# An attention kernel with bias: the first pair's bias chunk loaded last and added after the scores, and the second pair's first head copied straight from PSUM

## The chip, the cores and the metric

The kernel runs on one core of a Trainium2 chip. The metric is the device time of one execution in microseconds (us). A core has a matrix engine (PE, with its weight loads shown apart as PEld), VectorE (DVE), ScalarE (ACT), GpSimd (POOL) and SyncE (SP), each with its own instruction stream in a fixed order, and 16 DMA engines that serve the queues of all of them. Matmul results go to PSUM; everything else lies in SBUF.

## The reference

```python
batch, n_heads, seq_len, head_dim = 4, 8, 1024, 64
scores = (1 / sqrt(head_dim)) * q @ k.T + bias      # bias: [1, 1, 1024, 1024]
attn = exp(scores - max) / (sum(exp(scores - max)) + 1e-8)
out = attn @ v
```

All tensors are float32. There are 32 heads; one bias matrix serves all of them.

## The kernel before

**Tiling.** Heads are worked in 16 pairs. A *slot* is one query chunk c (128 queries) of one head h: a 128x1024 block of scores in one of three PSUM places (`pl`, two banks each). There are 256 slots. For 237 of them ACT takes the exponential of the whole block into a bf16 tile `E` (line 258); for 19, listed in `PLAN`, DVE works it out in six steps (lines 263 to 298). PE then multiplies it with V (`av`, line 312) into a PSUM bank `po` that collects up to 7 results, with V's 65th column of ones giving the sums, and DVE divides and stores (`evac`, lines 315 to 333).

**Scores that stay in PSUM.** A place keeps its sum from slot to slot. The first slot in a place (`start`) adds the bias to the score; each next slot of the same chunk adds its own head's score and takes away the one before. For that, an even head's operands `ke` and `qe` hold the head's own 64 rows and, in the other 64, those of the head before, negated in q; odd heads use `ko` and `qo` of the whole pair. `fill_half` (line 233) writes one bank: four matmuls of bias ("b", the bias chunk against 8 times the identity) or of scores ("s"). `fill` (line 246) writes both banks. Slots 0, 1 and 2 are the first head's chunks 0 to 2 in places 0 to 2.

**From memory to operands.** For each pair, K, Q and V are loaded by GpSimd's DMAs, which cast to bf16 (`load_k`, `load_q`, `load_v`, lines 141 to 167). PE transposes K and Q into a PSUM tile `px` under one of two tags, `xa` and `xb` (`transposes`, line 182), shared with the `po` banks. DVE copies `px` into `ko` or `qo` (`copy_out`, line 195), and from these the 64-row halves are copied into `ke` and `qe` (`double`, line 203; by DVE, GpSimd or, in later pairs, by DMA). V is copied into `vall` (line 493).

**The start** (lines 335 to 392) is written out by hand. Pair 0's q (three chunks), K (two halves) and bias chunk 0 come as float32 through SP's and ACT's queues: q and K's halves on SP, the bias on ACT. GpSimd clears `qz[0]` and `qs` (lines 350, 351; 64x1024 each) and then issues bias chunks 1 and 2, K and Q of pairs 1 and 2, and V of pair 0. DVE casts q and K's first half, ACT casts the bias and K's second half. PE transposes, DVE copies `qz` and `ko`. The bias matmuls of slot 0 go ahead of its scores, and its exponential runs as two halves; the bias matmuls of slot 1 stand between the two score halves of slot 0.

**The rest** is ordered by a planner in the kernel's own Python (lines 394 to 814). It keeps a clock for each engine (`t_pe`, `t_act`, `t_dve`, `t_pool`, in its own nanoseconds, from 9300, 9900, 9600 and 9000), estimates of each step's cost and of each load's landing (`raw_at`, `vland_at`, `t_dma`), and takes at each step what can begin first; work waiting for DVE lies in `dve_q` as (time ready, priority, cost, action), and a smaller priority goes first. What it writes out is a fixed order for each engine: on the chip an instruction waits for its data, and everything behind it on that engine waits too. GpSimd's loads after the start wait until the load five places earlier has landed (`issue`, line 463; the `tick` copies at line 468).

Transposes of a pair's piece are a candidate for PE (lines 646 to 675); behind them `run` (line 665) queues `copy_out` and then `doubles` (line 511), and frees the tag when the whole copy is done. Pair 1's first pieces are K (all 8 chunks) and Q (3 chunks); its even head is head 2, whose slots are 6, 7 and 8.

Of the kernel before, what the change touches and what calls it, by code (L numbers as in the profile page):

```python
# [11 lines left out]
ALU = mybir.AluOpType  # L12
# [4 lines left out]
def kernel(  # L17
# [13 lines left out]
    nc = tc.nc  # L31
    B, H, S, D = q.shape
# [6 lines left out]
    qf = q.rearrange("b (g t) (p c) d -> (b g) p t (c d)", t=2, p=P)  # L39
# [13 lines left out]
    C0 = 3  # L53
# [36 lines left out]
    slots = []  # L90
# [72 lines left out]
    def load_v(pr):  # L163
        lands[pr, "v"] = vland.tile([P, 2, NCH, D], BF, name="v16")
        nc.gpsimd.dma_start(out=lands[pr, "v"].rearrange("p t c d -> p t (c d)"),  # L165
                            in_=vf[pr].rearrange("p t c d -> p t (c d)"))
        return lands[pr, "v"][:1, 1, NCH - 1, D - 1:]
# [14 lines left out]
    def transposes(pr, which, c0, n, tag, px=None):  # L182
        if px is None:
            px = ps_x.tile([P, n, P], BF, tag=tag, name="px")
        for c in range(n):
            if (pr, which, c0) in raws:
                nc.tensor.transpose(px[:, c, :], raws[pr, which, c0][:, c].rearrange("p t d -> p (t d)"), ident[:])  # L187
                continue

            for t in range(2):  # L190
                nc.tensor.transpose(px[t * D:(t + 1) * D, c, :], lands[pr, which, c0][:, t, c, :], ident[:],  # L191
                                    tile_position=(0, t * D))
        return px
# [9 lines left out]
    def double(pr, which, c0, n, part, w):  # L203
# [7 lines left out]
        else:  # L211
            w.tensor_scalar(to[("qe", "qe", "qs", "qz")[part]][rows, cs, :], t["qo"][rows, cs, :], -1.0, 1.0,
                            op0=ALU.mult, op1=ALU.mult)

    def negate(pr):

        t = (raws[pr, 0, 0] if 0 in BESIDE else lands[pr, 0, 0]).rearrange("p t c d -> p (t c d)").rearrange("p (c x) -> p c x", x=P)
        nc.vector.tensor_scalar(t, arrs[pr]["qo"][:], -1.0, 1.0, op0=ALU.mult, op1=ALU.mult)
        return t
# [10 lines left out]
            return t["ko"], t["qz"] if pr in first_pair else t["qs"]  # L230
        return (t["ko"], t["qo"]) if h % 2 else (t["ke"], t["qe"])

    def fill_half(s, b, what):

        x, c, h, start = slots[s]
        kk, qq = operands(s)
        for i in range(4):
            kc = 4 * b + i
            to = places[x][:, b, i * P:(i + 1) * P]
            if what == "b":  # L240
                nc.tensor.matmul(to, braw[:, c, :].rearrange("p (kp kc) -> p kc kp", kc=NCH)[:, kc, :], ident8[:],  # L241
                                 start=i == 0, stop=False, skip_group_check=True)
            else:
                nc.tensor.matmul(to, kk[:, kc, :], qq[:, c, :], start=False, stop=True, skip_group_check=True)  # L244

    def fill(s):
        for what in "bs" if slots[s][3] and s > 1 else "s":
            for b in range(2):
                fill_half(s, b, what)

    etile = {}

# [82 lines left out]
    with tc.manual_schedule():  # L335

        half = NCH // 2
        nc.sync.dma_start(out=q0f[:], in_=qf[0][:, :, :C0 * D].rearrange("p t (c d) -> p t c d", d=D))
        nc.scalar.dma_start(out=b0f[:], in_=bf_[:, 0, :])
        for i in range(2):  # L340
            nc.sync.dma_start(out=k0f[:, :, i * half:(i + 1) * half].rearrange("p t c d -> p t (c d)"),
                              in_=kf[0][:, :, i * half * D:(i + 1) * half * D])
        nc.vector.memset(zeros, 0.0)
        nc.vector.memset(warm[:], 0.0)
        nc.vector.memset(sgn[:D, :], -1.0)
# [2 lines left out]
        make_identity(nc, ident[:])  # L348

        nc.gpsimd.memset(qz[0][D:, :, :], 0.0)  # L350
        nc.gpsimd.memset(qs[D:, :, :], 0.0)
        for c in (1, 2):
            load_b(c)
        load_k(1)
# [1 line left out]
        load_k(2)  # L356
        load_q(2, slice(0, NCH))
        load_v(0)
        for i in range(10):
            nc.tensor.matmul(places[2][:, 0, :], zeros[:, :P], zeros, start=True, stop=True)  # L360

# [7 lines left out]
        nc.vector.tensor_scalar(ident8[:], ident[:], 1.0 / scale, None, op0=ALU.mult)  # L369
        nc.vector.tensor_copy(qr0.rearrange("p c t d -> p t c d"), q0f[:])  # L370
        nc.vector.tensor_copy(kr0[0].rearrange("p c t d -> p t c d"), k0f[:, :, :half])
        nc.scalar.copy(braw[:, 0, :], b0f[:])
        nc.scalar.copy(kr0[1].rearrange("p c t d -> p t c d"), k0f[:, :, half:])

        pq = transposes(0, 0, 0, C0, "xa")
        pk = transposes(0, 1, 0, half, "xb")
        pk2 = places[2].bitcast(BF)[:, 1, :half * P].rearrange("p (c x) -> p c x", x=P)
        nc.vector.tensor_scalar(t0["qz"][:D, :C0, :], pq[:D], 1.0, None, op0=ALU.mult)
        copy_out(0, 1, 0, half, pk)
        for i in range(2):  # L380
            fill_half(0, i, "b")
        transposes(0, 1, half, half, None, px=pk2)
        copy_out(0, 1, half, half, pk2)
        copy_out(0, 0, 0, C0, pq)
        fill_half(0, 0, "s")
        exp(0, 0, 1)
        for i in range(2):
            fill_half(1, i, "b")
        fill_half(0, 1, "s")
        exp(0, 1, 1)  # L390
        double(0, 1, 0, NCH, 1, nc.vector)
        double(0, 0, 0, C0, 1, nc.vector)

# [38 lines left out]
        TR, SWITCH = 56, 190  # L432
        LATE, QCOST = 2, 4400
        flight = []
        LAG, AVG = 7, 247
        E1, E2 = 1400, 1700
        free_lands, loads, loads_v = set(), list(range(EARLY, NP)), []
# [70 lines left out]
            else:  # L508
                bias_at[pr] = issue(0, E2, 5, load_b, pr)

        def doubles(pr, which, c0, n, t2, urgent):
            if not which and pr >= EARLY:
                def run(t3):
                    to = negate(pr)
                    last = parts(pr, 0)[-1]
                    for x in parts(pr, 0):
                        key = (("qe", "qe1", "qs", "qz")[x], pr + (x == 1), 0)
                        sp_q.append((t3 + 430 + L_DVE, lambda t4, x=x, key=key: copy(pr, x, key[0][:2], to, key, t4, x == last)))
                dve_q.append((t2, 0.2 if urgent else 2, 430, run))
                return  # L520
            for x in parts(pr, which):
                key = (("ke", "ke1")[x], pr + (x == 1)) if which else (("qe", "qe1", "qs", "qz")[x], pr + (x == 1), c0)
                if which and (pr >= EARLY or x == 1 and pr >= 2):
                    sp_q.append((t2 + L_DVE, lambda t3, x=x, key=key: copy(pr, x, "ke", arrs[pr]["ko"], key, t3)))
                elif which or urgent:
                    cost = (130 if which else 240) + 38 * n

                    def run(t3, x=x, key=key, cost=cost):
                        double(pr, which, c0, n, x, nc.vector)
                        ready[key] = t3 + cost + L_DVE  # L530
                    dve_q.append((t2, (0.2, 0.4, 0.4, 0.2)[x] if urgent else 2, cost, run))
                else:
                    double(pr, which, c0, n, x, nc.gpsimd)
                    pool(t2)
                    ready[key] = pool(0, 125 * n + 100) + 300
# [40 lines left out]
        def pe_cands():  # L576
# [69 lines left out]
            if pieces:  # L646
                pr, which, c0, n = pieces[0]
                need = need_at[pr, which, c0]
                ring = pr + linked(pr) - RING
                lag = len([s for s in avq[:NE] if s in e_at])  # L650
                if ((pr, which, c0) in raw_at and next_fill >= need - AHEAD and (ring < 0 or last_slot[ring] < next_fill)
                        and (lag < 4 or need - next_fill < 8)):
                    f, tag = min((x_free[y], y) for y in x_free)
                    r = max(f, raw_at[pr, which, c0])
                    cost = n * TR + SWITCH * (pr < EARLY or which not in BESIDE)
                    urgent = need - next_fill < 12
                    if r < 1e11:
                        def do(t, pr=pr, which=which, c0=c0, n=n, tag=tag, cost=cost):
                            x_free[tag] = 1e12
                            pieces.pop(0)  # L660
                            px = transposes(pr, which, c0, n, tag)
                            if pr < EARLY and which == 0 and c0 == 0:
                                freed(pr, t)

                            def run(t2):
                                copy_out(pr, which, c0, n, px)
                                done = t2 + 60 * n + (180 if which else 300)
                                x_free[tag] = done + L_DVE
                                if which:
                                    ready["ko", pr] = done + L_DVE  # L670
                                else:
                                    ready["qo", pr, c0] = done + L_DVE
                                doubles(pr, which, c0, n, done, urgent)
                            dve_q.append((t + cost + L_PE, 0 if urgent else 2, 60 * n + (180 if which else 300), run))
                        out.append((max(t_pe, r), cost, do, 2 if next_fill < need - 12 else 0.5, 0))
            return out

# [167 lines left out]
```

## Time and profile before

| what | value |
|---|---|
| median of 3 runs | 232.69 us (232.66 to 232.89) |
| profiled execution | 232.87 us, span 230.8 us |
| PE / PEld busy | 222.4 us (96%) / 209.8 us (91%) |
| ACT busy | 221.3 us (96%), x242 |
| DVE busy | 197.3 us (85%) |
| POOL busy | 64.5 us (28%) |
| mean granted PE clock | 0.997 |
| DMA | 29.75 MB, mean 129 GB/s |

The span runs from the first to the last instruction of the core. A row of a timeline or of a group gives start and length in us, the engine, the source line, the operation and its tiles (output <- input), the count, and in brackets the idle time ahead of it and what ended it. The chain of waits gives the work that ended last, each piece with its start and length; "issue" is time in which the engine waited for nothing that the profile shows. A DMA row gives the queue: q0 is GpSimd's, q1 is SP's and q10 is ACT's. The busy share of a queue can go over 100%, since packets overlap. PE's busy time is modelled and overlaps, so a busy PE is not PE at its peak.

Where the prediction speaks of single starts, of packets or of landings, they are the trace's records of single instructions, packets and semaphores.

### The profile page before, as it was taken

Reading aid. Unit: us, or ns where it says so; the run is one execution under the profiler, and the core shown is the slowest. Engines: PE = TensorE matmul, PEld = TensorE weight load, DVE = VectorE, ACT = ScalarE, POOL = GpSimd, SP = SyncE. Lnnn points to the kernel's source line nnn. Section 1 sums busy time; section 2 is a strip of 40 time slices with the busy share of each in tenths; the row PEclk is TensorE's granted clock in tenths of the full one; section 3 lists DMA queues with packets and bytes.
Section 4 is the critical chain, followed back from the end, with each engine's and each line's share of the span. In section 5 each row is a group of like instructions: output and inputs, shape, how many; then the busy total and the mean of one; then the engine's idle time right before and its main releaser. Section 6 shows DMA issues by size and latency. Waiting matters only on the chain.

```text
span 230.8 us, 10695 instructions
## 1 busy us (share of the span) xinstructions
PE 222.4 (96%) x4671; PEld 209.8 (91%) x4671; DVE 197.3 (85%) x294; ACT 221.3 (96%) x242; POOL 64.5 (28%) x115
## 2 busy tenths in 40 slices
PE   6999999999999999999999999999999999999993
PEld 2779998999999999998999999999998999999992
DVE  3595678799988997989889789899999899999993
ACT  3799999999999999999999999999999999999994
POOL 8816655167444444313364010000000000000000
PEclk9999999999999999999999999999999999999998
DMA  6999999999999999989899864111111112112212
GB/s 201 212 205 225 216 228 213 195 120 121 161 193 150 146 178 153 176 193 147 140 253 196 186 123 114 38 37 43 43 36 48 45 43 65 53 26 71 65 37 63
DMA packets 55645, 29.75 MB, mean 129 GB/s; under 512 B 31856, under 2 KB 51952, under 8 KB 55600
## 3 DMA queue, kind: packets, MB, share of 16 engines
q0 software_dynamic: 30336, 14.06, 49.0%
q1 hardware_dynamic: 24832, 14.43, 22.6%
q8 instruction: 36, 0.59, 1.0%
q10 hardware_dynamic: 432, 0.59, 0.9%
q14 instruction: 9, 0.07, 0.1%
HBM read 29.36 MB, written 8.39 MB: 164 GB/s over the span
## 4 chain that ended last, share of the span: by engine, by line
PE 36%; ACT 28%; issue 13%; DMA 11%; DVE 7%; POOL 3%; SPq 1%; DVEq 0%; ACTq 0%; POOLq 0%
ACT E L258 28%; PE pl L244 21%; PE po L312 10%; DMA v<-in_v_dram 6%; DMA k<-in_k_dram 4%; PE px L191 2%; PE pl L241 2%; DVE ob L322 2%; DVE dt L290 1%; DVE dy L275 1%; DVE de L295 1%; SPq L694 1%; POOL k L145 1%; POOL q L155 1%; DMA out_dram<-ob 1%
## 5 line engine op out<-in xcount | busy, mean ns | idle before, releaser
L258 ACT ACTIVATE E<-pl 128x1024 bf16<-128x1024 f32 (+1 forms) x238 | 218.1, 1124 | 1.9 <-PE pl L244 1.7
L312 PE MATMUL po<-vall,E 128*128 128x65 bf16 x1896 | 92.0, 194 | 0.7 <-ACT E L258 0.7
L312 PEld LDWEIGHTS <-E 128*128 128x128 bf16 x1896 | 77.5, 98 | 1.8 <-ACT E L258 1.1
L244 PE MATMUL pl<-qo,ko 128*128 128x128 bf16 x1024 | 77.0, 219 | 1.2 <-ACT E L258 0.6
L244 PEld LDWEIGHTS <-ko 128*128 128x128 bf16 x1160 | 69.6, 98 | 4.4 <-issue 1.2
L244 PE MATMUL pl<-qe,ke 128*128 128x128 bf16 x888 | 66.1, 219 | 0.6
L244 PEld LDWEIGHTS <-ke 128*128 128x128 bf16 x888 | 53.4, 98 | 3.4
L275 DVE TENSOR_SCALAR dy<-pl 128x1024 int32<-128x1024 f32 x19 | 23.2, 1222 | 3.4 <-PE pl L244 2.4
L322 DVE TENSOR_TENSOR ob<-po,rs 128x448 f32<-128x448 f32 (+2 forms) x40 | 23.3, 581 | 2.7 <-DMA out_dram<-ob 0.8
L284 DVE SCALAR_TENSOR_TENSOR dt<-df 128x1024 f32<-128x1024 f32 x19 | 23.2, 1220 | 0.3
L295 DVE SCALAR_TENSOR_TENSOR de<-dy,dt 128x1024 uint16<-128x1024 int32 x19 | 23.2, 1219 | 0.1
L287 DVE SCALAR_TENSOR_TENSOR df<-dt,df 128x1024 f32<-128x1024 f32 x19 | 23.1, 1219 | 0.1
L290 DVE SCALAR_TENSOR_TENSOR dt<-df,dt 128x1024 f32<-128x1024 f32 x19 | 23.1, 1219 | 0.1
L138 POOL DMA_DIRECT2D q<-in_q_dram x18 | 16.1, 898 | 5.8 <-PE po L312 4.2
L165 POOL DMA_DIRECT2D v<-in_v_dram x16 | 11.3, 704 | 12.0 <-DVE rs L320 7.5
L199 DVE COPY ko<-px 128x1024 bf16<-128x1024 bf16 (+1 forms) x16 | 10.7, 671 | 4.4 <-PE px L191 4.1
L201 DVE TENSOR_SCALAR qo<-px,sgn 128x1024 bf16<-128x1024 bf16 (+2 forms) x18 | 12.4, 687 | 2.1 <-PE px L187 1.7
L320 DVE RECIPROCAL rs<-po 128x7 f32<-128x7 f32 (+3 forms) x42 | 8.2, 195 | 7.0 <-PE po L312 6.8
L280 DVE TENSOR_SCALAR df<-dy 128x1024 f32<-128x1024 uint16 x19 | 13.0, 687 | 0.1
L241 PE MATMUL pl<-ident,braw 128*128 128x128 bf16 x136 | 11.5, 228 | 0.1
L145 POOL DMA_DIRECT2D k<-in_k_dram x15 | 10.7, 711 | 2.6 <-PE pl L244 1.0
L493 DVE COPY vall<-v 128x1024 bf16<-128x1024 bf16 x16 | 7.0, 438 | 4.3 <-DMA v<-in_v_dram 4.2
(55 smaller groups left out, 124.9 us busy)
## 6 DMA issues: line engine op xcount, KB each, us to landing
v<-in_v_dram POOLq DMA_DIRECT2D x16, 256.0 KB, 6.3
k<-in_k_dram POOLq DMA_DIRECT2D x15, 256.0 KB, 6.1
out_dram<-ob SPq DMA_DIRECT2D x35, 96.0 KB, 3.3
ke<-ko SPq DMA_DIRECT2D x22, 128.0 KB, 4.2
out_dram<-ob SPq DMA_DIRECT2D x40, 64.0 KB, 2.2
q<-in_q_dram POOLq DMA_DIRECT2D x18, 128.0 KB, 4.6
out_dram<-ob SPq DMA_DIRECT2D x68, 32.0 KB, 3.0
qe<-q SPq DMA_DIRECT2D x17, 128.0 KB, 4.1
```

The lines of the kernel that those rows point to most:

```text
L138: nc.gpsimd.dma_start(out=t[:, :, y, :], in_=(qf, kf)[x][pr][:, y].rearrange("p (c d) -> p c d", d=D))
L145: nc.gpsimd.dma_start(out=t.rearrange("p t c d -> p t (c d)"), in_=kf[pr])
L241: nc.tensor.matmul(to, braw[:, c, :].rearrange("p (kp kc) -> p kc kp", kc=NCH)[:, kc, :], ident8[:], start=i == 0, stop=False, skip_group_ ...
L244: nc.tensor.matmul(to, kk[:, kc, :], qq[:, c, :], start=False, stop=True, skip_group_check=True)
L258: nc.scalar.activation(e[:, i:i + n].rearrange("p b x -> p (b x)"), places[slots[s][0]][:, i:i + n].rearrange("p b x -> p (b x)"), ACTF.Ex ...
L275: w.tensor_scalar(t["y"][:], places[slots[s][0]].rearrange("p b x -> p (b x)"), scale * LOG2E * 65536.0, 127.0 * 65536.0, op0=ALU.mult, op ...
L284: w.scalar_tensor_tensor(t["t"][:], t["f"][:], -G, t["f"][:], op0=ALU.add, op1=ALU.mult)
L287: w.scalar_tensor_tensor(t["f"][:], t["t"][:], Q, t["f"][:], op0=ALU.mult, op1=ALU.add)
L290: w.scalar_tensor_tensor(t["t"][:], t["f"][:], V, t["t"][:], op0=ALU.add, op1=ALU.mult)
L295: w.scalar_tensor_tensor(etile[s].bitcast(U16).rearrange("p c q -> p (c q)"), t["y"][:], 1.0 / 512.0, t["t"][:], op0=ALU.mult, op1=ALU.add)
L312: nc.tensor.matmul(po[:, j + i, :], etile[s][:, kc, :], vall[:, slots[s][2] % VR, kc, :], start=j + i + kc == 0, stop=kc == NCH - 1, skip_ ...
L322: nc.vector.tensor_tensor(ob[:, :n, :], po[:, :n, :D], rs[:, :n, :].to_broadcast([P, n, D]), op=ALU.mult)
```

## The change

Loads: K's first half moves to ACT's queue, ahead of everything there; SP's queue takes q, K's second half, and then bias chunk 0 in two halves of 512 columns. The cast of the bias is split in the same way and goes behind that of K's second half on ACT. The clearing of `qs` goes behind the seven loads on GpSimd.

Slots 0 to 2: the score matmuls come first and the bias matmuls second, and slot 0's exponential is one instruction over both banks. Slot 1's bias matmuls leave the hand-written start and stand in its own fill.

Pair 1: its K and first Q piece are copied from PSUM into the 64 rows of `ke` and `qe` directly (`direct`); the whole copies into `ko` and `qo` are queued once both are done, and the double of that half is left out.

```diff
+    def direct(pr, which, c0, n, px):
+        to = arrays(pr)["ke" if which else "qe"][:D, c0:c0 + n, :]
+        if which:
+            nc.vector.tensor_copy(to, px[:D])
+        else:
+            nc.vector.tensor_scalar(to, px[:D], 1.0, None, op0=ALU.mult)
...
     def fill(s):
-        for what in "bs" if slots[s][3] and s > 1 else "s":
+        order = ("sb" if s < 3 else "bs") if slots[s][3] else "s"
+        for what in order:
             for b in range(2):
-                fill_half(s, b, what)
+                fill_half(s, b, what, len(order) > 1 and what == order[0])
...
-        nc.sync.dma_start(out=q0f[:], in_=qf[0][:, :, :C0 * D].rearrange("p t (c d) -> p t c d", d=D))
-        nc.scalar.dma_start(out=b0f[:], in_=bf_[:, 0, :])
+        for i, e in enumerate((nc.scalar, nc.sync)):
+            if i == 0:
+                nc.sync.dma_start(out=q0f[:], in_=qf[0][:, :, :C0 * D].rearrange("p t (c d) -> p t c d", d=D))
+            e.dma_start(out=k0f[:, :, i * half:(i + 1) * half].rearrange("p t c d -> p t (c d)"),
+                        in_=kf[0][:, :, i * half * D:(i + 1) * half * D])
         for i in range(2):
-            nc.sync.dma_start(out=k0f[:, :, i * half:(i + 1) * half].rearrange("p t c d -> p t (c d)"),
-                              in_=kf[0][:, :, i * half * D:(i + 1) * half * D])
+            nc.sync.dma_start(out=b0f[:, i * 512:(i + 1) * 512], in_=bf_[:, 0, i * 512:(i + 1) * 512])
...
-        nc.gpsimd.memset(qs[D:, :, :], 0.0)
         for c in (1, 2):
             load_b(c)
...
         load_v(0)
+        nc.gpsimd.memset(qs[D:, :, :], 0.0)
...
-        nc.scalar.copy(braw[:, 0, :], b0f[:])
         nc.scalar.copy(kr0[1].rearrange("p c t d -> p t c d"), k0f[:, :, half:])
+        for i in range(2):
+            nc.scalar.copy(braw[:, 0, i * 512:(i + 1) * 512], b0f[:, i * 512:(i + 1) * 512])
...
-        for i in range(2):
-            fill_half(0, i, "b")
         transposes(0, 1, half, half, None, px=pk2)
         copy_out(0, 1, half, half, pk2)
         copy_out(0, 0, 0, C0, pq)
-        fill_half(0, 0, "s")
-        exp(0, 0, 1)
         for i in range(2):
-            fill_half(1, i, "b")
-        fill_half(0, 1, "s")
-        exp(0, 1, 1)
+            fill_half(0, i, "s", True)
+        for i in range(2):
+            fill_half(0, i, "b", False)
+        exp(0)
...
-            for x in parts(pr, which):
+            for x in [y for y in parts(pr, which) if y not in done]:
...
-                                doubles(pr, which, c0, n, done, urgent)
-                            dve_q.append((t + cost + L_PE, 0 if urgent else 2, 60 * n + (180 if which else 300), run))
+                                doubles(pr, which, c0, n, done, urgent, (0,) * early_pair)
+                            early_pair = pr == 1 and c0 == 0
+                            copying = 60 * n + (180 if which else 300)
+                            def head(t2):
+                                direct(pr, which, c0, n, px)
+                                done = t2 + 60 * n + 180
+                                ready[("ke", 1) if which else ("qe", 1, 0)] = done + L_DVE
+                                behind.append((done, 0.1, copying, run))
+                                if len(behind) == 2:
+                                    dve_q.extend(behind)
+                            if early_pair:
+                                dve_q.append((t + cost + L_PE, 0, 60 * n + 180, head))
+                            else:
+                                dve_q.append((t + cost + L_PE, 0 if urgent else 2, copying, run))
```

The planner's constants (its starting clocks, the loads' estimates, `PLAN`, `DUE`) stay as they are.

More of the change, by code (lines that the diff above doesn't have):

```diff
@@ L231, in operands, with fill_half @@
         return (t["ko"], t["qo"]) if h % 2 else (t["ke"], t["qe"])
-    def fill_half(s, b, what):
+    def fill_half(s, b, what, first):
         x, c, h, start = slots[s]
@@ L241, in fill_half @@
                 nc.tensor.matmul(to, braw[:, c, :].rearrange("p (kp kc) -> p kc kp", kc=NCH)[:, kc, :], ident8[:],
-                                 start=i == 0, stop=False, skip_group_check=True)
+                                 start=first and i == 0, stop=not first, skip_group_check=True)
             else:
-                nc.tensor.matmul(to, kk[:, kc, :], qq[:, c, :], start=False, stop=True, skip_group_check=True)
+                nc.tensor.matmul(to, kk[:, kc, :], qq[:, c, :], start=first and i == 0, stop=not first, skip_group_check=True)
     def fill(s):
-        for what in "bs" if slots[s][3] and s > 1 else "s":
+        order = ("sb" if s < 3 else "bs") if slots[s][3] else "s"
+        for what in order:
             for b in range(2):
-                fill_half(s, b, what)
+                fill_half(s, b, what, len(order) > 1 and what == order[0])
     etile = {}
@@ L377 @@
         pk2 = places[2].bitcast(BF)[:, 1, :half * P].rearrange("p (c x) -> p c x", x=P)
+        transposes(0, 1, half, half, None, px=pk2)
         nc.vector.tensor_scalar(t0["qz"][:D, :C0, :], pq[:D], 1.0, None, op0=ALU.mult)
         copy_out(0, 1, 0, half, pk)
-        for i in range(2):
-            fill_half(0, i, "b")
-        transposes(0, 1, half, half, None, px=pk2)
         copy_out(0, 1, half, half, pk2)
         copy_out(0, 0, 0, C0, pq)
-        fill_half(0, 0, "s")
-        exp(0, 0, 1)
         for i in range(2):
-            fill_half(1, i, "b")
-        fill_half(0, 1, "s")
-        exp(0, 1, 1)
+            fill_half(0, i, "s", True)
+        for i in range(2):
+            fill_half(0, i, "b", False)
+        exp(0)
         double(0, 1, 0, NCH, 1, nc.vector)
@@ L434 @@
         flight = []
+        behind = []
         LAG, AVG = 7, 247
@@ L509, in early, with doubles @@
                 bias_at[pr] = issue(0, E2, 5, load_b, pr)
-        def doubles(pr, which, c0, n, t2, urgent):
+        def doubles(pr, which, c0, n, t2, urgent, done=()):
             if not which and pr >= EARLY:
```

## The prediction

> **What bounds the kernel now.** I read the page's busy shares first: PE 96%, ACT 96%, so two engines are full and a saving counts only where both can use it. Then the timeline of ACT, which runs 238 exponentials (two of them halves):
>
> ```profile
> 5.22 1.04 ACT L372 CAST braw<-df 128x1024 bf16<-128x1024 f32 x1 [2.51 <-DMA df<-in_bias_dram]
> 6.73 0.62 ACT L373 CAST de<-dt 128x512 bf16<-128x512 f32 x1 [0.46 <-DMA dt<-in_k_dram]
> 8.06 0.60 ACT L258 ACTIVATE E<-pl 128x512 bf16<-128x512 f32 x1 [0.71 <-PE pl L244]
> 9.13 39.45 ACT L258 ACTIVATE E<-pl 128x512 bf16<-128x512 f32 x43 [0.47 <-PE pl L244]
> ```
>
> The reader sees ACT waiting at the start (2.51, 0.46, 0.71, 0.47 us) and then 39 us without a shown wait. Single starts in the trace: slot 1 at 9.62, slot 2 at 10.53, slot 6 at 14.15, slot 11 at 18.66, slot 30 at 36.03; back to back they are 0.904 apart. From slot 1 on, ACT loses 4.4 us over 0.905 per slot, in some 17 gaps.
>
> So an earlier first exponential should shorten the run one for one, unless something tied to a fixed time stands behind it. The DMA rows say that something does. In 10 to 40 us queue q0 alone (GpSimd's loads) is over full:
>
> ```profile
> q0 software_dynamic: 5581, 5.36, 109.3%
> ```
>
> and engines wait for its landings; the chain of waits from 24 to 36 us, and the waits of 8 to 50 us, show where:
>
> ```profile
> 26.24 6.89 DMA v<-in_v_dram
> 33.13 0.02 issue
> 33.15 0.43 DVE vall L493
> 33.58 0.32 DVE qs L212
> 33.90 0.12 DVE rs L320
> 34.02 0.02 issue
> 34.04 0.57 DVE ob L322
> 34.61 0.14 issue
> 34.75 0.64 PE px L191 x16
> 35.38 1.00 PE pl L244 x16
> ```
> ```profile
> DVE vall L493 <- DMA v<-in_v_dram: 4.2, 5, 1.4
> ```
> ```profile
> 17.00 0.64 PE L191 MATMUL px<-ident,k 128*64 128x128 bf16 x16 [0.20 <-DMA k<-in_k_dram]
> 17.57 0.62 PE L244 MATMUL pl<-qo,ko 128*128 128x128 bf16 x8
> ```
>
> V of pair 4 lands at 33.13; DVE, in its fixed order, then copies it and only afterwards evacuates the bank that PE needs for transposes at 34.75; the fills of slots 30 and 31 stand behind these, and slot 30 starts at 36.03, already 0.21 late (1.112 after its forerunner). K of pair 3 lands at 16.96 and holds PE the same way. From 34.75 to 48.7 the chain is PE alone, without idle.
>
> **The change, part by part.**
>
> *Loads.* Landings before: bias 0.75+4.5 = 5.2, q 0.76+4.6 = 5.4, K's halves 6.0 and 6.7. After, q (192 KB, SP) and K's first half (256 KB, ACT) go first, then K's second half and two bias halves of 256 KB on SP, issued at about 1.25, 1.76 and 2.23 (0.46 to 0.47 each, as the K rows); SP has nothing else until 14.22. The bytes, 1216 KB, are the same. The DMA view gives 194 GB/s in 2 to 3 us, 343 in 3 to 4, 356 after; a landing follows the last packet by 0.35. So q and the first K half (0.46 MB) at 3.8+0.35 = 4.15, the second half 4.9, the bias 5.65 and 6.4.
>
> *The first slot.* DVE: cast of q 0.60 and of K 0.43 from 4.15, to 5.18; qz copy 0.35, ko copy 0.42, to 5.95. ACT: cast of K's second half 0.62, 4.9 to 5.52; bias halves at 5.65 and 6.4, a cast of 0.62 each by the 128x512 row (1.24 where the whole took 1.04), done 7.02. PE: transposes 0.40 to 5.95, DVE copy 0.42 to 6.4, the score half 0.4 to 6.85, the last four bias matmuls 0.35 to 7.4. The whole exponential then starts near 7.45. Before, its equivalent is 9.62-0.904 = 8.72. Gain here 1.27.
>
> *Slots 1 and 2.* Each needs a bias chunk of q0. GpSimd issues them 0.95 earlier (the qs memset, 0.95, goes behind seven loads; qs is first written at 33.49, and K of pair 3, next behind the memset, keeps its 7.95). But before 5.77 q0 moved nothing, and HWDGE packets last till 6.37: I keep the landings at 7.94 and 9.15. Bounds: 0 to 0.95 earlier. Eight bias matmuls take 0.66, so slot 1 starts near 8.65 and slot 2 near 9.85. Gain left 0.68; scores or bias first costs PE the same matmuls.
>
> *Pair 1.* K lands at 10.43 (4.37+6.1). PE is there at 10.45 instead of 10.86; transposes 0.64. The 64-row copies from PSUM are not in the trace: ke lies between 0.42 (64 rows, SBUF) and 0.69 (128 rows, PSUM), I take 0.69, as it reads the same PSUM row length; qe 0.35, the qz copy's row. So ke 11.8, qe 12.3, the fill of slot 6 12.4 to 12.85, wanted by 13.4. By the old order, ko 0.69, ke 0.42, qo 0.40, qe 0.25, it would be 13.05 to 13.5: the direct copies are worth 0.1 here. They cost DVE 0.69+0.35-0.42-0.25 = 0.37, and 0 to 0.4 by the bounds. The whole copies (0.69, 0.40) run behind, so both px tags come free some 0.7 later and K of pair 2 is transposed about as much later; pair 2 is first filled at 18.29 and its last double ends at 17.28. DVE's own wait of 1.10 before V of pair 1 at 19.92 covers it; without that cover it would be 0.37.
>
> *What then is late.* The loads behind carry the same bytes through a full queue, so their landings stay (0 to 0.2 earlier). At 16.96 PE stands ahead of K of pair 3: slot 11's fill ends at 18.03, the exponential starts at 18.08 and not at 18.66-0.68 = 17.98. Gain 0.58. At 33.13 DVE stands before V of pair 4: 0.43+0.41+0.18+0.56 with their overlap put the transposes at 34.7 again, and slot 30 at 36.03 again. Gain 0, with the order as it is. From there PE's chain has no slack.
>
> *The order itself.* Lines 394 to 814 work out a fixed order from estimates. With them by hand, slot 6's fill was ready at 14,067 (filled 14,724 against ACT free at 14,533), now at 13,309: the plan's ACT loses 0.19 less, its loads stay. So up to 0.19 more PE work may stand ahead of the held transposes; bounds 0 and 0.58. I take 0.1, near the lower end, since the trace's only row for that place is the hold itself.
>
> **Sum.** 232.87 (profiled execution: span 230.8 and 2.07 around it) less 0.1 is 232.8; the median of the runs, 232.69, lies 0.18 lower: **232.6**. About 0.2% (0.47 us) is what a measurement of this kernel can tell from no change.
>
> **The rivals.**
>
> *The gain is kept.* If the new order puts the evacuation before the V copy at 33.13 (its PE result is there by 33.8 already), nothing holds PE at 34.75 and 0.58 to 0.9 stays: 231.7 to 232.1, 231.9 as one number. For it: DVE is idle 1.15 there. Against: the plan still waits for V by a fixed estimate. Chance 0.27.
>
> *The new order fits worse (slower).* Place: 34.75 to 48.7, where PE is the chain and ACT's gaps are 0.21, 0.42, 0.17 and 0.32. There one pair's transposes (0.57) set one fill too early stop ACT by what the fill's slack lacks: the gaps show 0.17 to 0.42 a time. Two more such misplacements, about 0.35 each, bring +0.7: 233.3, up to 234. It decides from the point where the added gaps exceed what is kept of the 0.68. For it: 17 such gaps already exist. Chance 0.20.
>
> *The bias halves land late (slower).* q0's first packets may be ready long before 5.77, held only by the longer HWDGE queues. From 4.8 to 5.7 the view of the queues reads
>
> ```profile
> q1 hardware_dynamic: 336, 0.33, 106.0%
> q10 hardware_dynamic: 1, 0.00, 0.1%
> ```
>
> and has no row of q0, 1.6 us after its first issue at 3.16. If q0 shared packet by packet from 4.9 (issue 2.3 plus 2.6, the delay shown), the 11 or so bias packets left on each engine, near 0.105 each, would alternate with 0.173 ones: 11 x 0.278 = 3.1, landing near 8.4, exponential 0 near 9.5, 0.8 late; PE's waits at 16.19, 17.0 and 34.75 (0.33, 0.37, 0.39 of lost issue time) absorb part, and +0.5 remains: 233.2. It decides when q0 starts before the second half is through. Chance 0.11. Against it: at 5.8, 6.0, 6.1 and 6.2 us the trace has 15, 11, 6 and 1 engines on q1 and 2, 7, 11 and 15 on q0, as if each took q0 up only when q1 was drained. For it: q1 and q10 did share packet by packet in 2.5 to 4.5 us. The Trainium skill (DMA: Bandwidth & Descriptors, Queues, rings and completion order) says that each DMA engine goes round its queues packet by packet, which is this rival. By that rule the time would be 233.2; first come, first served, as q0's late start looks, leaves the forecast.
>
> **The numbers.** My forecast (232.3 to 232.95) has 0.42, the gain kept 0.27, the two slower ones 0.31. Of the forecast, 0.03 falls on the faster and 0.02 on the slower side of the bound: faster 0.30, same 0.37, slower 0.33. The range 231.9 to 233.5 leaves out the lowest third of the kept gain (0.09) and the upper third of the slower cases (0.10).
>
> **What would show it.** Loads: bias landings at 5.65 and 6.4, or one beyond 8. First slot: an exponential near 7.45, slot 2 near 9.85, slot 6 near 13.4. Pair 1: a 64-row copy near 0.69. The hold: slot 30 at 36.0 and PE idle some 0.6 to 0.9 before the transposes near 34.75. I am wrong if slot 30 starts before 35.6 and the lead lives to the end, or if ACT's gaps beyond slot 30 add up to over 0.5 more than before.

## The result and the profile after

| what | before | after |
|---|---|---|
| median of 18 runs each | 233.0 us (232.56 to 234.46) | 234.65 us (232.93 to 237.53) |
| ratio, after to before | | 1.0059, interval 1.0034 to 1.0084 |
| profiled execution | 232.87 us, span 230.8 us | 233.26 us, span 231.2 us |

The changed kernel is slower by some 0.6%. (The ratio leaves one disturbed run out and is not the quotient of the medians.) Two things have to be told apart. The profiled execution is one of the shortest: 233.26 us, only 0.4 above before. But 14 of the 18 runs lie above 233.9 us, against 2 of 18 before. A cause must explain both, and the profile of after shows only the first.

The page of after, its span and its first row of busy times: the engines are as full as before.

```profile
span 231.2 us, 10699 instructions
PE 222.1 (96%) x4671; PEld 209.7 (91%) x4671; DVE 197.7 (86%) x294; ACT 221.7 (96%) x242; POOL 65.6 (28%) x115
```

ACT's timeline from 5 to 12 us in the profiled execution of after (L386 is the cast of K's second half, L388 that of the bias halves, L268 the exponential):

```profile
5.59 0.62 ACT L386 CAST de<-dt 128x512 bf16<-128x512 f32 x1 [2.82 <-DMA dt<-in_k_dram]
6.31 1.24 ACT L388 CAST braw<-df 128x512 bf16<-128x512 f32 x2
8.36 3.83 ACT L268 ACTIVATE E<-pl 128x1024 bf16<-128x1024 f32 x4 [0.80 <-PE pl L249]
```

The first exponential starts at 8.36 in one piece; before, the halves ran at 8.06 and 9.13. Slots 1, 2 and 6 start at 9.30, 10.25 and 13.88 against 9.62, 10.53 and 14.15, so the lead is 0.28 where the forecast had 0.68. By slot 24 it has shrunk to 0.19. Then it goes, in two places that the next views show. DVE and PE, from 28 to 32 us:

```profile
28.83 0.43 DVE L506 COPY vall<-v 128x1024 bf16<-128x1024 bf16 x1 [1.54 <-DMA v<-in_v_dram]
29.18 0.68 DVE L199 COPY ko<-px 128x1024 bf16<-128x1024 bf16 x1
```
```profile
29.91 0.64 PE L191 MATMUL px<-ident,q 128*64 128x128 bf16 x16
```

The copy of V in the profile of before:

```profile
28.60 0.43 DVE L493 COPY vall<-v 128x1024 bf16<-128x1024 bf16 x1 [1.44 <-DMA v<-in_v_dram]
```

DVE waits 1.54 us for V of pair 3, which lands at 28.81 (28.58 before); the copy of K behind it ends at 29.86, and PE begins Q's transposes 0.05 later, after a gap of 0.31 (counted from start to start, less the 0.06 that these matmuls stand apart). Between slots 24 and 25 a lead of 0.19 becomes a lag of 0.15. And the chain of waits from 24 to 36 us:

```profile
26.38 6.90 DMA v<-in_v_dram
...
33.29 0.43 DVE vall L506
...
34.19 0.57 DVE ob L332
...
34.89 0.64 PE px L191 x16
```

It is the chain of before, 0.14 later at its end (34.75 then): V of pair 4 lands at 33.27, not 33.13, and slot 30 starts at 36.18 instead of 36.03. At 42.2 PE stops once more and slot 38 is 0.42 late; from slot 43 to the end the lag stays at 0.45. (From 38 on, the numbers of slots count ACT's exponentials in order, up to 236, here and in the expectations; the slots that DVE works out are left out, so that 38 is slot 39 of the plan.) That is the short execution. What fills the long ones came out of the experiments.

### The profile page after: what moved, and what is told of

The parts are those of the page before. It is cut to its first block, busy times and chain, and to the rows that moved or that the text cites. A ratio compares the mean times of both kernels' runs of the same rounds, so it can differ in the third digit from the quotient of the medians.

```text
span 231.2 us, 10699 instructions
## 1 busy us (share of the span) xinstructions
PE 222.1 (96%) x4671; PEld 209.7 (91%) x4671; DVE 197.7 (86%) x294; ACT 221.7 (96%) x242; POOL 65.6 (28%) x115
## 4 chain that ended last, share of the span: by engine, by line
PE 36%; ACT 28%; issue 13%; DMA 10%; DVE 8%; POOL 3%; DVEq 0%; ACTq 0%; POOLq 0%
ACT E L268 28%; PE pl L252 21%; PE po L322 10%; DMA v<-in_v_dram 6%; DMA k<-in_k_dram 4%; PE px L191 2%; PE pl L249 2%; DVE ob L332 2%; DVE dt L300 1%; DVE df L297 1%; DVE dy L285 1%; DVE de L305 1%; DVE df L290 1%; DVE dt L294 1%; POOL q L155 1%
## 5 line engine op out<-in xcount | busy, mean ns | idle before, releaser
L268 ACT ACTIVATE E<-pl 128x1024 bf16<-128x1024 f32 x237 | 218.4, 1111 | 1.9 <-PE pl L249 0.8
L481 POOL COPY tick<-q 1x1 bf16<-1x1 bf16 x13 | 5.5, 421 | 25.7 <-DMA q<-in_q_dram 25.7
```

The lines of the kernel that those rows point to most:

```text
L268: nc.scalar.activation(e[:, i:i + n].rearrange("p b x -> p (b x)"), places[slots[s][0]][:, i:i + n].rearrange("p b x -> p (b x)"), ACTF.Ex ...
```

## The experiments

The first four kernels ran on one chip, the next four on another, and the last four on that one again. A lag or lead below is a slot's start less the same slot's start in the profile of before. The kernel before was measured again beside each group; 12 of 35, 5 of 23 and 2 of 16 of its runs lie above 233.9 us.

**1. The changed kernel again.** No edit.

> The changed kernel once more, for a second profile and times on this chip. Theory A (the plan's order): its time is 0.4 to 0.5 us over the kernel before in every execution, as the two profiles show (slot 236 starts 0.45 later), and the rest of the 1.4 us between the medians is scatter of both. Theory B (the start is at times much slower: PE's clock is released later, or one DMA engine lags): the executions spread over 3 us or more, with a lower mean granted clock in the longer ones, while the kernel before spreads over less than 1.5 us.

Measured: median 234.73 us of 12 (232.89 to 238.31), ratio 1.0049 [1.0013, 1.0085]; 7 of 12 above 233.9. The profiled execution, 233.28 us, was a short one again: lead 0.31 at slot 2, lag 0.18 at slot 32 and 0.45 at the end. So the loss repeats, and a profile is likely to miss it. Theory B is met in part: the runs spread over 5.4 us, and four of the seven long ones have a mean granted clock of 0.989 to 0.993 (0.995 to 1.0 in the other eight); but the kernel before spreads over 6.1 us here.

**2. The new start alone**, with pair 1 copied in the old way.

```diff
...
-                            if early_pair:
-                                dve_q.append((t + cost + L_PE, 0, 60 * n + 180, head))
-                            else:
-                                dve_q.append((t + cost + L_PE, 0 if urgent else 2, copying, run))
+                            dve_q.append((t + cost + L_PE, 0 if urgent else 2, 60 * n + (180 if which else 300), run))
```

> The new loads, the bias after the scores, the qs memset behind; pair 1 as before and with it the old plan. Theory A: slots 25 and 38 lose their new gaps (0.34 and 0.28), the lead of 0.3 at slot 1 is held up at slot 30 as before, so 0 to -0.2 us against the kernel before. Theory B: the slow executions stay: median 0.8 to 1.2 us over the kernel before, with a spread of 3 us.

Measured: 233.47 us median (232.85 to 235.2), ratio 1.001 [0.998, 1.004]; 5 of 12 above 233.9, about the share of the kernel before, so neither theory's number is met. In its profile (234.04 us) the lead is 0.42 at slot 2, 0.10 at slot 24 and gone at slot 25; the lag is 0.08 up to slot 121. The +1.10 at slot 132 is another thing, shown in the last section.

**3. The direct copies alone**, with the start, its loads and slots 0 to 2 as before.

```diff
-        for i, e in enumerate((nc.scalar, nc.sync)):
...
+        nc.sync.dma_start(out=q0f[:], in_=qf[0][:, :, :C0 * D].rearrange("p t (c d) -> p t c d", d=D))
+        nc.scalar.dma_start(out=b0f[:], in_=bf_[:, 0, :])
...
+        nc.gpsimd.memset(qs[D:, :, :], 0.0)
         for c in (1, 2):
             load_b(c)
...
-        nc.gpsimd.memset(qs[D:, :, :], 0.0)
```

> The old start with the new pair 1 and its new plan. Theory A: the gaps at slots 25 and 38 are there, +0.4 to +0.6 us against the kernel before. Theory B: 0 to +0.4 us, and a spread as narrow as that of the kernel before.

Measured: 233.59 us median (232.9 to 236.01), ratio 1.0019 [0.9988, 1.0049]; 4 of 12 above 233.9, again the share of the kernel before. In its profile (232.90 us) all slots from 0 to 29 lead by about 0.18, already at slot 0, so this is not the direct copies' doing; at slot 34 and at the end the lag is 0.02 and 0.03. No gain or cost of the direct copies that lasts can be seen; the interval would hide one of up to 0.5%.

**4. The whole change, but GpSimd's loads start as late as before.**

```diff
         nc.gpsimd.memset(qz[0][D:, :, :], 0.0)
+        nc.gpsimd.memset(qs[D:, :, :], 0.0)
         for c in (1, 2):
             load_b(c)
...
-        nc.gpsimd.memset(qs[D:, :, :], 0.0)
```

> The changed kernel with the qs memset back in front of GpSimd's loads, so that these are issued 0.95 us later. If the earlier loads cross the bias halves (third theory, packet by packet), the bias halves land earlier and the time falls by 0.3 us or more; if they only wait behind them, as in the profile (q0 starts at 5.79 in both), the time is that of the changed kernel within 0.2 us. Theories A and B say the latter.

Measured: 233.24 us median (232.76 to 233.6), ratio 0.9975 [0.9948, 1.0002]. None of 12 is above 233.9, where the changed kernel beside it had 7. Its profiled execution, 233.36 us, looks like that of after (lead 0.26 at slot 2, lag 0.52 at slot 38): this edit does not shorten the short execution; the long ones are gone. Between these two kernels the place of one instruction of 0.95 us on GpSimd makes the medians 233.24 and 234.73. As the kernel before had 12 long runs of 35 beside them, a part of the 0 may be luck.

**5 and 6. The changed kernel twice more, to catch a long execution in a profile.** No edit.

> The changed kernel, one more profile. More than half of its executions lie over 233.9 us, so this may show one. If the long executions come from late output stores between 60 and 135 us (VectorE waits for its output buffer, as the start-only kernel's profile shows for 2.2 us at 129.9), a long one has such waits of 1 us or more and slot 236 late by as much; if they come from PE's clock, its record begins after 5 us or is broken and the lateness is there before slot 10.

> As the look before: a profile of the changed kernel, to see a long execution. Late stores: waits for the output buffer between 60 and 135 us. Clock: late before slot 10.

Measured: 233.1 and 234.71 us, the second a long one. Its last bias half lands at 8.67 (6.79 in the first), slot 0 starts at 10.11, and the lag is 1.46 at slot 2 and 1.87 at the end. The semaphore of that half shows how: a load reports once for each of 16 DMA engines. In the 234.71 execution 14 reports come between 6.20 and 6.79, and the last two at 8.65 and 8.67; in the 233.1 execution all 16 come between 5.97 and 6.79.

The packets of the 234.71 execution show what held the two. Of the 256 bias packets most take 0.084 us and follow each other every 0.080 us on an engine. Two of them, at 5.11 and 5.14, take 1.32 us each. When the other engines are through, seven bias packets are still to come on each of two engines, in two regular series that begin at 6.583 and 6.614. q0 moves by then, and now one bias packet of 0.096 us passes every 0.246 us on each, with a packet of q0 in the time between (the trace names no engine; that these are two is read from the two series). Seven times the added 0.166 is 1.2 us, an estimate of what the sharing cost on top of the slow packets. It was q0's first packet at 5.77, the time of before, that they met, so the earlier issue isn't needed to explain this one execution.

**7. The clearing of `qs` on DVE**, with GpSimd's loads as early as in the change.

```diff
-        nc.gpsimd.memset(qs[D:, :, :], 0.0)
...
+        nc.vector.memset(qs[D:, :, :], 0.0)
```

> The changed kernel with the clearing of qs on VectorE at the start, and none on GpSimd: all of GpSimd's loads 0.95 us earlier than in the kernel before, K of pair 3 too. If loads issued that much earlier make the long executions, the median stays at 234.5 or more; if the memset behind the seven loads makes them (K of pair 3 behind it on GpSimd), it falls to 233.0 to 233.4 with a spread under 1 us.

Measured: 233.07 us median (232.69 to 236.8), ratio 0.9997 [0.9964, 1.003]; 4 of 12 above 233.9. Issue at 2.26; in the profiled execution, a short one, the bias half lands at 6.77 and the end lags 0.17. By the early issue the expectation was a median of 234.5 or more, and I would have expected as many long executions, here and in experiment 2 (5 of 12), as in the change (23 of 34 over all its runs). That is missed: the median sides with the rival, the place of the memset behind the loads, though the spread of 4 us does not. Why there are fewer is open.

**8. The new start alone, with the late issue.**

```diff
         nc.gpsimd.memset(qz[0][D:, :, :], 0.0)
+        nc.gpsimd.memset(qs[D:, :, :], 0.0)
...
-        nc.gpsimd.memset(qs[D:, :, :], 0.0)
...
-                            if early_pair:
-                                dve_q.append((t + cost + L_PE, 0, 60 * n + 180, head))
-                            else:
-                                dve_q.append((t + cost + L_PE, 0 if urgent else 2, copying, run))
+                            dve_q.append((t + cost + L_PE, 0 if urgent else 2, 60 * n + (180 if which else 300), run))
```

> The new start alone (pair 1 and the plan as before), with the qs memset back in front of the loads. By the hold at slot 30 its fastest executions are those of the kernel before within 0.2 us; if the memset's place makes the long executions, its median is under that of the start-only kernel, at 232.8 to 233.2, with no execution over 234.

Measured: 233.29 us median (232.71 to 235.19), ratio 0.9993 [0.9965, 1.0021]; 2 of 12 above 233.9, where none was expected. Even here the bias half may come late on one engine (15 reports by 6.72, the last at 7.15), and slot 2 has a lag of 0.07 in place of a lead.

**9. GpSimd's loads still earlier**: the clearing of `qz[0]` goes to DVE, so the first issue is at 1.44. If the early issue is the cause, the loss must now come every time and be larger.

```diff
+        nc.vector.memset(qz[0][D:, :, :], 0.0)
...
-        nc.gpsimd.memset(qz[0][D:, :, :], 0.0)
```

> The changed kernel with the clearing of qz[0] on VectorE too, so that GpSimd's loads are issued another 0.95 us earlier, near 1.4. In the long execution that was seen, two of the 16 DMA engines went between the last bias half and GpSimd's first load packet by packet, and that half landed at 8.67 and not at 6.9. If the early issue brings this about, it happens in most executions here: bias half at 8 us or later in the profile, median 235 us or more. If the place of the memset, or chance, does it, the median is 233.1 to 234.7.

Measured: 238.1 us median of 6 (236.21 to 238.59), ratio 1.018 [1.0127, 1.0233]; every run is long. ACT's timeline from 5 to 12 us and the DMA view from 4.5 to 5.5 us (queue: packets, MB, share of 16 engines):

```profile
5.49 0.62 ACT L386 CAST de<-dt 128x512 bf16<-128x512 f32 x1 [2.74 <-DMA dt<-in_k_dram]
7.88 0.62 ACT L388 CAST braw<-df 128x512 bf16<-128x512 f32 x1 [1.78 <-DMA df<-in_bias_dram]
9.55 0.62 ACT L388 CAST braw<-df 128x512 bf16<-128x512 f32 x1 [1.05 <-DMA df<-in_bias_dram]
11.34 1.02 ACT L268 ACTIVATE E<-pl 128x1024 bf16<-128x1024 f32 x1 [1.16 <-PE pl L249]
```
```profile
q0 software_dynamic: 60, 0.12, 67.2%
q1 hardware_dynamic: 139, 0.16, 46.2%
```

Both queues move side by side, from 4.45 on, when all 256 packets of the bias halves are still to come. Now all 16 reports of the last half are late (8.94 to 9.53), not two. Slot 0 starts at 11.34, slot 2 is 4.22 late, and the end lags 5.19. Not all of that is the wait itself. PE's bias matmuls of slot 0, and below them those of slot 1 in after:

```profile
10.23 1.07 PE L249 MATMUL pl<-ident,braw 128*128 128x128 bf16 x8 [2.70 <-ACT braw L388]
```
```profile
8.60 0.66 PE L249 MATMUL pl<-ident,braw 128*128 128x128 bf16 x8
```

PE waits 2.70 us for the cast of the late half. From 9.45 to 16.27 us its granted clock is 0.5, and eight matmuls take 1.07 us there in place of 0.66. After the waits of 0.96 to 1.47 us at the same place in experiments 6, 11 and 12 the granted clock stays at 1.0. All six runs here have a mean granted clock of 0.982 to 0.991.

**10. GpSimd's loads later**: `qs` cleared twice in front of them, so the first issue is at 4.16.

```diff
         nc.gpsimd.memset(qz[0][D:, :, :], 0.0)
+        nc.gpsimd.memset(qs[D:, :, :], 0.0)
+        nc.gpsimd.memset(qs[D:, :, :], 0.0)
...
-        nc.gpsimd.memset(qs[D:, :, :], 0.0)
```

> The changed kernel with the qs memset in front of the loads, and twice, so that they are issued near 4.1 us. If sharing with the bias halves makes the long executions: none over 234, and since q0 begins near 5.6 whether it is issued at 2.3 or 3.2, the floor stays at 232.8 to 233.2. If q0's start hangs on its issue, bias chunk 1 lands near 9 and all executions are 0.5 to 1 us longer.

Measured: 234.4 us median (234.03 to 237.36), ratio 1.0059 [1.0027, 1.009]. The bias halves are on time (6.88), and ACT's timeline shows what is late instead:

```profile
9.57 1.02 ACT L268 ACTIVATE E<-pl 128x1024 bf16<-128x1024 f32 x1 [0.22 <-PE pl L249]
10.84 1.94 ACT L268 ACTIVATE E<-pl 128x1024 bf16<-128x1024 f32 x2 [0.25 <-PE pl L249]
```

Bias chunks 1 and 2 land at 8.79 and 10.04 (8.11 and 9.36 in after), so slots 1 and 2 wait for them; slot 2 lags 0.32 and the end 1.61. q0's first packet is no later than elsewhere (5.64), but 37 of its 2 KB packets up to 8.4 us take over 0.2 us each, where after has none. So both ends, 1.44 and 4.16, lose in every run. Between 2.27 and 3.16 experiments 1 and 4 speak for the later issue; experiment 7, at 2.26, does not.

**11 and 12. The changed kernel two last times.** No edit.

> A further profile of the changed kernel. By the sharing: where the time is over 234, the last bias half lands after 7.5 us and slot 0 starts after 9; where it is under 233.5, that half lands before 7. Another cause would show a long execution with slot 0 at 8.4.

> A further profile of the changed kernel, read as the one before it.

Measured: 233.47 and 235.14 us, last bias half at 8.05 and 8.59, again by two late reports of 16 (7.87 and 8.05; 8.17 and 8.59), with 14 there by 6.92 and 6.86. ACT from 5 to 11.2 us in the 235.14 execution, to be held against the rows of after above:

```profile
5.56 0.62 ACT L386 CAST de<-dt 128x512 bf16<-128x512 f32 x1 [2.80 <-DMA dt<-in_k_dram]
6.31 0.62 ACT L388 CAST braw<-df 128x512 bf16<-128x512 f32 x1
8.62 0.62 ACT L388 CAST braw<-df 128x512 bf16<-128x512 f32 x1 [1.69 <-DMA df<-in_bias_dram]
10.04 1.97 ACT L268 ACTIVATE E<-pl 128x1024 bf16<-128x1024 f32 x2 [0.80 <-PE pl L249]
```

And the DMA view of 6.8 to 7.4 us, first of after (its only row of a queue), then of this execution:

```profile
q0 software_dynamic: 74, 0.13, 114.4%
```
```profile
q0 software_dynamic: 67, 0.12, 104.9%
q1 hardware_dynamic: 5, 0.01, 5.0%
```

The rows agree up to the first cast of the bias and part there: ACT waits 1.69 us for the second bias half, of which a few packets still pass among q0's. The whole kernel then starts 1.40 behind before (slot 2) and ends 2.32 behind; 0.5 of that comes at slot 100, where PE issues late for no reason that the profile shows.

Put together, the six profiles of the changed kernel, by landing of the last bias half: 6.79, 6.87, 6.91, 8.05, 8.59, 8.67 us, with times of 233.1, 233.28, 233.26, 233.47, 235.14, 234.71 us. The three late ones are the three longest. In the three short ones q0's first packet comes at 5.64 to 5.79, with 43 to 62 of the 256 bias packets still to start; in experiments 11 and 12 at 5.27 and 5.30, with 179 and 149. Experiment 6 has 5.77 and 54, and yet two late engines, those of the two slow packets; so an earlier first packet is not the whole condition. In experiments 11 and 12 q0's first packet takes 0.52 and 0.81 us, and from 5.8 and 6.1 on there are again two series of bias packets 0.246 us apart. The length of 0.096 us marks the packets that alternate with q0: 14 to 17 of 256 have it in the three late profiles, 0 to 2 in the three short ones, and 218 in experiment 9.

The granted clock on record tells something of the runs that no profile shows. Of the 30 runs of the change in its two series 11 have a mean of 0.993 or less, and they took 234.95 to 238.31 us. In experiments 2 and 7, with the same early issue, it is 1 and 2 of 12. In the three with the issue of before, 3, 4 and 8, it is none of 36, in experiment 10 1 of 12, and in the kernel before 2 of the 74 runs beside the experiments. A clock lost after a late bias half, as experiment 9's profile shows it, fits these counts; no profile of the changed kernel shows such a run.

## Why the prediction failed

**The cause is the rival that I gave 0.11: the bias halves land late**, in each of the two executions above 234.5 us that a profile of the change caught. The step that failed is the reading of q0's late start. "As if each took q0 up only when q1 was drained" took what one profile showed for a rule, and so the earlier issue had no price in the sum. In the short executions it still looks so: there 0 to 2 of the 256 bias packets alternated with q0's. But it is no rule. Issued at 1.44 (experiment 9), q0 moves from 4.45 on, side by side with all the bias packets. Issued at 2.27, it found two engines with bias packets left in three of six profiles, and there a bias packet passed every 0.246 us in place of every 0.080. The Trainium skill (DMA: Bandwidth & Descriptors, Queues, rings and completion order), as the prediction cited it, has each engine go round its queues packet by packet. The 0.246 us, room for one packet of each queue, agree with it. Nor does q0 begin a fixed time after its issue: issued at 1.44, 2.27, 3.16 and 4.16, it first moves at 4.45, 5.27 to 5.79, 5.52 to 5.86 and 5.64. What holds it until 5.3 to 5.9 at the three later issues stays open, and with it how the issue at 2.27 makes late halves more frequent; that it does is argued from experiments 4 and 9 and from the counts of runs.

The rival's own numbers came close in place: a landing near 8.4 (8.05 to 8.67 measured) and an exponential near 9.5 (9.49, 10.04 and 10.11 in the three profiles with late halves). But it is not all 16 engines that share, and not in every execution: two late ones are enough, since a load counts as landed with its last report, and whether there are any differs from run to run.

**"PE's waits absorb part" of the lateness was wrong too.** The working let 0.8 late shrink to +0.5. Instead 1.46 at slot 2 became 1.87 at the end (experiment 6), 1.40 became 2.32 (experiment 12, with the 0.5 at slot 100), 4.22 became 5.19 (experiment 9, with the lower clock up to 16.27); only 0.87 shrank, to 0.64 (experiment 11). So 233.47, 234.71 and 235.14 us stand where the rival said 233.2. A lead and a lag are not alike here, and my reading of it, which no run tested, is this: the lead is lost where PE or DVE waits for a load; a lag finds the loads there, but PE, 96% busy, has little room to catch up.

**The size of the first slot was off.** The five loads land at 4.59 and 4.89 (forecast 4.15), 5.57 (4.9), and 6.29 and 6.91 (5.65 and 6.4): 0.4 to 0.7 late each. A landing is the last of 16 reports; the middle one of K's first half came at 4.27. The casts ended at 7.55, not 7.02, and the exponential came 0.80 behind them, not 0.43. Hence 8.36 and not 7.45. Slot 2 is less off, 10.25 for 9.85, with bias chunk 2 landing at 9.36 for 9.15: the early issue had not brought it forward, as assumed.

**Right, for the short executions:** that the lead would not outlive the loads of V. Slot 30 starts at 36.18 (forecast 36.03), after PE's gap of 0.35, counted as above, before the transposes at 34.89 (forecast 0.6 to 0.9, for a larger lead). Experiments 1, 2, 4, 5 and 7, each with a lead of 0.26 to 0.44 at slot 2, end 0.08 to 0.56 behind (experiment 2 read ahead of slot 132). The place is not always slot 30: in experiments 1, 5 and 7 V of pair 4 lands 0.16 to 0.26 earlier than before, slot 30 keeps a lead of 0.16 to 0.23, and it goes or shrinks at slot 32; in 1 and 5 PE stops 0.19 and 0.26 us there without a wait that the profile shows. Not foreseen: the hold one pair earlier, at slot 25, and the stop at slot 38. The rival of the worse order, at +0.7, has the direction of the short executions (+0.4 in after) but not their cause: from 17 us on each pair's transposes stand behind as many fills in after as before.

**Right, too,** was the price of the direct copies, in DVE's timeline from 10 to 14 us of after:

```profile
11.43 0.68 DVE L219 COPY ke<-px 64x1024 bf16<-64x1024 bf16 x1 [2.72 <-PE px L191]
12.27 0.35 DVE L221 TENSOR_SCALAR qe<-px 64x384 bf16<-64x384 bf16 x1 [0.16 <-PE px L191]
```

0.68 and 0.35 for 0.69 and 0.35: the copy of 64 rows of K out of PSUM took 0.68, that of all 128 behind it 0.67. DVE's busy time grew by 0.4, as worked out (0.37).

**What stays open.** Five of the 18 runs of after are above 235.2 us, longer than any profile caught, all with a granted clock of 0.988 to 0.993; a late half and then a lower clock, as in experiment 9, is likely and not shown. Why experiments 2 and 7 have fewer long executions than the change is open, and so is the cause of the runs of before above 233.9 (21 of 92 in all). The stop at slot 38 (0.24 to 0.61 us in which PE waited for nothing shown, near 42.2 in after) appears in after and in experiments 1, 4, 6, 7, 9, 10 and 12 and not in the others. A 16 KB instruction load begins at 39.7 in after and at 40.0 in experiment 4, and at 39.3 to 39.4 in the profiles of before and experiments 2, 3, 5 and 8, without the stop; but in experiment 11 it begins at 39.6, without the stop too, so a late fetch is a guess. No version beats the kernel before: the best, experiment 4, has 1.0002 in its interval.

## What to carry to other kernels

When a load is issued earlier, ask what it will now share engines with: bytes that are wanted first should be through before the next queue wakes, and one profile in which a queue woke late is no promise that it always will. A load is as late as its slowest DMA engine, so take the last of the 16 reports, and read several executions, since a profile of a short one hides what the median shows. In this kernel, whose engines are full, a late start was mostly carried to the end, while an early one was lost by slot 38.

## What the runs showed of the hardware

- From issue to first packet GpSimd's queue took 3.0 to 3.5 us at issue times of 1.44 and 2.27, 2.4 to 2.7 at 3.16, 1.5 at 4.16, and 1.4 at 110.22 in the kernel before.
- In three of six profiles of one kernel, two of the 16 DMA engines were 1.0 to 1.9 us later with the same load than the other 14, and in the other three none.
- Where two queues had packets at one engine, they alternated: a bias packet every 0.246 us (experiments 6, 11 and 12), every 0.080 us without the other queue.
- After PE had waited 2.70 us in experiment 9, it was granted half its clock for 6.8 us; after waits of 0.96 to 1.47 us in three other profiles it was not.
- A store can hold DVE long after it was issued. The waits of 118 to 142 us in experiment 2, and the chain there:

```profile
DVE ob L332 <- DMA out_dram<-ob: 2.2, 1, 2.2
```
```profile
122.73 6.91 DMA out_dram<-ob
...
130.57 0.64 PE px L191 x16
```

  The store takes 6.91 us where the page of this execution gives 1.9 to 4.1 as medians; DVE waits for its buffer, PE for DVE, and slot 132 is 1.1 late.
